# Three of eight K pairs in seven products, with two sums made by a transfer, in the SwiGLU of an encoder block

## The chip, the core and the metric

The kernel runs on one core of a Trainium2 chip. The metric is device time in microseconds of one execution. PE (TensorE) multiplies matrices into PSUM; PEld is its weight load, DVE (VectorE) and ACT (ScalarE) are the two elementwise engines, POOL (GpSimd) and SP (SyncE) are used here mostly to issue transfers (DMAs). Each engine runs its own instructions in order and waits on semaphores for the others.

## The reference

One encoder layer on x of 256 x 2048 in f32: two kinds of attention side by side, cross attention, and a SwiGLU. The change is in the SwiGLU alone:

```python
    hf = rms_norm(x, g_ffn[layer])
    x = x + (jax.nn.silu(hf @ w_gate[layer]) * (hf @ w_up[layer])) @ w_down[layer]
return rms_norm(x, g_final)
```

w_gate and w_up are 2048 x 5632, w_down 5632 x 2048.

## The kernel before

Every f32 product is made from three products in a rounded f32 format (fp32r): each operand is split into a high part (ACT copies with rounding, L97) and a low part (DVE subtracts, L98), and `mm` (L87 to L91) multiplies high by high, high by low and low by high. `split_into` does one split; `weights` and `pair_raw` load weights.

The SwiGLU's 5632 hidden columns are cut into one narrow chunk of 512 and five wide chunks of 1024. They run in three groups (L757), and after each group its part of `w_down` is multiplied and added to the residual `x_res`. Group 0 begins with `narrow_chunk`: the gate product `ga` and the up product `ua` over 16 K tiles, with x^T before normalization (`x2T`); the row factor `rstdf` of the RMS norm is applied afterwards (L731 to L734), and h is transposed on PE (L286).

The wide chunks use x^T after normalization. `normalized_forms` makes it once, after the narrow chunk (L762): it spreads `rstdf` along rows (L692, L693), multiplies the four kept tiles of x^T by it (L697), splits them into `x2n` for plain pairs, and makes `x2f` for the others: four sums and differences of the four 128 x 128 blocks (L714 to L717) and their splits.

A wide chunk makes two wide products, gate and up, with `wide_project`. Each goes over 8 pairs of K tiles in the order `GU_ORDER`. For a plain pair (P) PE makes 8 products of 128 x 128 by 128 x 512, each three matmuls. For a W pair it makes 7 products of sums of blocks (a scheme of Strassen and Winograd): three go straight into the accumulators `accs`, four into PSUM tiles Q1, Q5, Q7 and Q6, which collect over all W pairs of the product and are combined once, after the last W (L677 to L681). Then each accumulator is added to its combination (L684). `accs` take the four banks of `pacc`, Q the four of `pps`, which the transposes also use.

A W pair needs four sums of weight blocks. The weights lie in HBM in the order of blocks 12, 11, 22, 21 (`SUMS`). SP loads the four (1 MB, into `wraw`, three buffers). DVE makes the first two sums in one instruction (L658: blocks 11 and 22, each plus block 12), the others with L662 and L663, all in one tile `tsum` with one buffer. Blocks 11 and 22, block 21, and the first two sums are split into tiles of `wh` and `wl` (four buffers each, handed out in turn, two for a plain pair and three for a W pair); the last two sums into `wh2` and `wl2` (one buffer).

The framework decides the order of instructions on each engine at build time from a simulated timeline (`schedule_with_timeline_sim`, L901), so the built order may differ from the source. Only the weight loads on SP are kept in program order. POOL has no work in the SwiGLU before the last group.

Of the kernel before, what the change touches and what calls it, by code (L numbers as in the profile page):

```python
# [11 lines left out]
F32 = mybir.dt.float32  # L12
# [4 lines left out]
ALU = mybir.AluOpType  # L17
AX = mybir.AxisListType

P = 128  # L20
# [15 lines left out]
NFC = FF // 512  # L36
NPC = (FF - 512) // 1024

GU_ORDER = "PPWPWPPP"

PLAIN, SUMS = ((0, 0), (0, 1), (1, 0), (1, 1)), ((0, 1), (0, 0), (1, 1), (1, 0))
EPS = 1e-6
# [30 lines left out]
def encoder_block(ctx: ExitStack, tc: tile.TileContext, a, out):  # L73
    nc = tc.nc
# [62 lines left out]
    def project(actT, pieces, before=None, fine=0):  # L137

        accs = [pacc.tile([P, 512], F32, name="acc", tag="acc") for _ in range(NT)]
        ncols = pieces[0].shape[2]  # L140
        nk = sum(src.shape[1] for src in pieces)
        kt = 0
        for i, src in enumerate(pieces):
            if before is not None:
                before(i)
            for w in weights(src, i < fine):
                x = actT(kt)
                for tt in range(NT):
                    mm(accs[tt][:, :ncols], x[:, tt * P:(tt + 1) * P], w, start=kt == 0, stop=kt == nk - 1)
                kt += 1  # L150
        return accs
# [211 lines left out]
    for tt in range(NT):  # L363
        c = ckvs[tt]
# [92 lines left out]
    for hg in range(2):  # L457
        t = act_tile(name="mixT")
# [95 lines left out]
    for tt in range(NT):  # L554
        n = nat("xk")
# [53 lines left out]
    wsum = ctx.enter_context(tc.tile_pool(name="wsum", bufs=1))  # L609


    def pair_raw(src):
        raw = wp.tile([P, 2048], F32, name="wraw", tag="wraw", bufs=3)
        raw = raw.rearrange("p (b c) -> p b c", b=4)
        tc.keep_in_program_order(nc.sync.dma_start(out=raw, in_=src))
        return raw

# [6 lines left out]
    def split_blocks(src, pool=None):  # L624
        w = w_tile(src.shape[1], pool)
        split_into(w, src)
        return w

    def wide_project(xk, forms, src, order):

        accs = [[pacc.tile([P, 512], F32, name="acc", tag="acc") for _ in range(2)] for _ in range(NT)]
        used = [[False] * 2 for _ in range(NT)]
        last_w = max(i for i, kind in enumerate(order) if kind == "W")
        first_w = order.index("W")
        Q = {}  # L640
        for i, kind in enumerate(order):
            stop = i == len(order) - 1
            raw = pair_raw(src[i])
            if kind == "P":
                w = [split_blocks(raw[:, 2 * k:2 * k + 2, :]) for k in range(2)]
                for tt in range(NT):
                    for oc in range(2):
                        for k in range(2):
                            mm(accs[tt][oc], xk(2 * i + k)[:, tt * P:(tt + 1) * P], w[k][:, oc, :],
                               not used[tt][oc], stop and k == 1)  # L650
                            used[tt][oc] = True
                continue
            f = forms[i]
            if i == first_w:
                Q = {q: ps_tile(f"q{q}") for q in (1, 5, 7, 6)}
            t = wsum.tile([P, 4, 512], F32, name="tsum", tag="tsum", bufs=1)
            b11 = split_blocks(raw[:, 1:3, :])
            nc.vector.tensor_tensor(out=t[:, 0:2, :], in0=raw[:, 1:3, :],  # L658
                                    in1=raw[:, 0:1, :].to_broadcast([P, 2, 512]), op=ALU.add)
            t13 = split_blocks(t[:, 0:2, :])  # L660
            b21 = split_blocks(raw[:, 3:4, :])
            nc.vector.tensor_tensor(out=t[:, 2, :], in0=t[:, 0, :], in1=raw[:, 2, :], op=ALU.add)  # L662
            nc.vector.tensor_tensor(out=t[:, 3, :], in0=t[:, 2, :], in1=raw[:, 3, :], op=ALU.add)  # L663
            t24 = split_blocks(t[:, 2:4, :], wsum)
            own = i == first_w, i == last_w
            A11, A12, A22, S5, S6, S7, S3 = [f[:, n, :] for n in range(7)]
            mm(Q[1], A11, b11[:, 0, :], *own)
            mm(accs[0][1], S3, b11[:, 1, :], False, stop)
            mm(Q[5], S5, t13[:, 0, :], *own)
            mm(Q[7], S7, t13[:, 1, :], *own)  # L670
            mm(accs[0][0], A12, b21[:, 0, :], False, stop)
            mm(Q[6], S6, t24[:, 0, :], *own)
            mm(accs[1][0], A22, t24[:, 1, :], False, stop)
            if i == last_w:
                res = [act.tile([P, 2, 512], F32, name=f"res{tt}", tag="act") for tt in range(NT)]
                q1, x, v, y = res[0][:, 0, :], res[0][:, 1, :], res[1][:, 0, :], res[1][:, 1, :]
                nc.scalar.copy(out=q1, in_=Q[1])  # L677
                nc.vector.tensor_tensor(out=v, in0=Q[6], in1=q1, op=ALU.subtract)
                nc.vector.tensor_tensor(out=x, in0=Q[5], in1=v, op=ALU.add)
                nc.vector.tensor_tensor(out=v, in0=v, in1=Q[7], op=ALU.subtract)  # L680
                nc.vector.tensor_tensor(out=y, in0=Q[5], in1=v, op=ALU.add)  # L681
        for tt, oc, op in ((0, 0, ALU.add), (0, 1, ALU.add), (1, 0, ALU.subtract), (1, 1, ALU.add)):
            r = res[tt][:, oc, :]
            nc.vector.tensor_tensor(out=r, in0=accs[tt][oc], in1=r, op=op)  # L684
        return res

    def normalized_forms():

        rb = nat("rb")
        rps = ps_tile("rps")  # L690
        for tt in range(NT):
            nc.vector.tensor_copy(out=rb[:, tt * P:(tt + 1) * P], in_=rstdf[:, tt:tt + 1].to_broadcast([P, P]))  # L692
            nc.tensor.transpose(out=rps[:, tt * P:(tt + 1) * P], in_=rb[:, tt * P:(tt + 1) * P], identity=ident)  # L693
        rrow = nat("rrow")
        nc.scalar.copy(out=rrow[:, :S], in_=rps[:, :S])
        for xr in x2raw:
            nc.vector.tensor_tensor(out=xr, in0=xr, in1=rrow[:, :S].unsqueeze(1).to_broadcast([P, 4, S]), op=ALU.mult)  # L697
        plain, forms = {}, {}
        t, n = None, 4
        for i, kind in enumerate(GU_ORDER):  # L700
            xr = x2raw[i // 2]
            ka, kb = i % 2 * 2, i % 2 * 2 + 1
            if kind == "P":
                if n == 4:
                    t, n = act_tile(name="x2n"), 0
                split_into(t[:, n:n + 2, :], xr[:, ka:kb + 1, :])
                plain[2 * i], plain[2 * i + 1] = t[:, n, :], t[:, n + 1, :]
                n += 2
                continue
            f = act_tile((P, 7, P), name="x2f")  # L710
            forms[i] = f
            s = nat("x2s").rearrange("p (n t) -> p n t", n=4)
            a11, a12, a21, a22 = xr[:, ka, :P], xr[:, kb, :P], xr[:, ka, P:], xr[:, kb, P:]
            nc.vector.tensor_tensor(out=s[:, 0, :], in0=a21, in1=a22, op=ALU.subtract)  # L714
            nc.vector.tensor_tensor(out=s[:, 1, :], in0=a11, in1=s[:, 0, :], op=ALU.subtract)
            nc.vector.tensor_tensor(out=s[:, 2, :], in0=a11, in1=a21, op=ALU.subtract)
            nc.vector.tensor_tensor(out=s[:, 3, :], in0=a12, in1=s[:, 1, :], op=ALU.subtract)  # L717
            split_into(f[:, 0:2, :], xr[:, ka:kb + 1, :P])
            split_into(f[:, 2, :], a22)
            split_into(f[:, 3:7, :], s)  # L720
        return plain.__getitem__, forms

    def narrow_chunk(c):

        ga = project(x2T, [a["w_gate0"][0, i] for i in range(4)])
        ua = project(x2T, [a["w_up0"][0, i] for i in range(4)])
        t = act_tile(name="hT")
        for tt in range(NT):
            r = rstdf[:, tt:tt + 1]
            sg = nat("sg")  # L730
            nc.scalar.activation(sg, ga[tt], AF.Sigmoid, scale=r)  # L731
            nc.vector.scalar_tensor_tensor(out=sg, in0=ga[tt], scalar=r, in1=sg, op0=ALU.mult, op1=ALU.mult)
            h = nat("h")
            nc.vector.scalar_tensor_tensor(out=h, in0=ua[tt], scalar=r, in1=sg, op0=ALU.mult, op1=ALU.mult)  # L734
            transposed(t, h, tt, 4)
        return [t]

    def wide_chunk(c):
        g = wide_project(x2n, x2f, a["w_gu"][c, 0], GU_ORDER)
# [18 lines left out]
    for gi, (c0, c1) in enumerate(groups):  # L758
        hT = []
        if gi == 0:  # L760
            hT += narrow_chunk(0)
            x2n, x2f = normalized_forms()  # L762
        for c in range(len(hT) + c0, c1, 2):
            hT += wide_chunk((c - 1) // 2)
        if gi == len(groups) - 1:
            gfb = [act.tile([P, 1024], F32, name="gfb", tag="act") for _ in range(2)]
            for c in range(2):
                nc.gpsimd.dma_start(out=gfb[c],
                                    in_=a["g_final"][:, c * 1024:(c + 1) * 1024].partition_broadcast(P))
        for oc in range(4):  # L770
# [6 lines left out]
            if oc < 3:  # L777
                add_out(project(xT, pieces), oc)
                for tt in range(NT):
# [3 lines left out]
                                            op=ALU.mult)  # L783
# [3 lines left out]
            n = 4 * len(pieces) - 6  # L787
# [117 lines left out]
```

## Time and profile before

| | us |
|---|---|
| median of 3 runs | 1186.28 |
| lowest and highest | 1185.59, 1188.68 |
| the profiled execution | 1185.42 |
| its span | 1183.6 |
| the forms and the join to the first wide chunk, on the timeline | 489 to 504 |
| two wide products without a narrow one, on the timeline | 912 to 997 |

The span is what the trace covers, from first to last instruction; the rest of the execution's time lies around it. A row of the timeline gives start and length in us, engine, line, operation, output and inputs; in brackets the idle time before it and what ended that. A row of a group ends with busy time in all, mean ns of one, and idle time before. The chain that ended last is followed back from the last instruction; its shares say which engine's work made up the time. Matmul ends are modelled, so PE's pace is better read from the starts of matmuls than from their lengths.

### The profile page before, as it was taken

How to read it: one execution, taken by the hardware profiler on the slowest of the kernel's cores; microseconds unless marked ns; L12 is line 12 of the kernel's file. 1: busy time of each engine (PE TensorE's matmuls, PEld its weight loads, DVE VectorE, ACT ScalarE, POOL GpSimd, SP SyncE). 2: the span in 40 equal slices, each digit the busy share in tenths (PEclk: the TensorE clock that was granted, in tenths of full speed). 3: DMA queues.
4: the chain of work that ended last, by engine and by line, in shares of the span. 5: the costliest groups of instructions: out<-in, count | busy, mean ns of one | idle time of the engine just before them, and what ended most of it. 6: DMA issues, size and time to landing. Idle time of an engine off the chain costs nothing.

```text
span 1183.6 us, 14683 instructions
## 1 busy us (share of the span) xinstructions
PE 1160.9 (98%) x5728; PEld 977.3 (83%) x5728; DVE 839.6 (71%) x1084; ACT 593.5 (50%) x830; POOL 66.0 (6%) x83
## 2 busy tenths in 40 slices
PE   8999999999999999799999999999999999999997
PEld 5889888888889988688888888888888887888887
DVE  6768766686867776788755787887546787887553
ACT  5746454454665555455443544544433554554452
POOL 7610000001000000000000000000000000000111
PEclk9999999999999999899999999999999999999999
DMA  8656425445755445445555556555555655755551
GB/s 292 237 181 214 143 107 178 167 154 194 281 201 178 143 147 187 164 148 180 210 209 180 181 207 207 186 179 213 192 199 182 209 178 178 249 180 212 182 207 74
DMA packets 33829, 222.16 MB, mean 188 GB/s; under 512 B 3920, under 2 KB 4304, under 8 KB 9056
## 3 DMA queue, kind: packets, MB, share of 16 engines
q1 hardware_dynamic: 32544, 217.24, 52.2%
q0 software_dynamic: 928, 3.20, 0.9%
q8 instruction: 45, 0.74, 0.2%
q10 hardware_dynamic: 288, 0.79, 0.2%
q14 instruction: 24, 0.20, 0.1%
HBM read 219.11 MB, written 2.10 MB: 187 GB/s over the span
## 4 chain that ended last, share of the span: by engine, by line
PE 94%; DMA 2%; DVE 2%; ACT 1%; issue 1%; SPq 0%; POOLq 0%; POOL 0%; DVEq 0%; ACTq 0%
PE acc L90 28%; PE acc L89 27%; PE acc L91 27%; PE pt L286 2%; PE q L90 2%; PE q L89 2%; PE q L91 2%; DMA wraw<-in_w_in_q 1%; DVE wl L98 1%; DMA xres<-in_x 1%; PE ppt L432 1%; PE psc L91 1%; PE psc L90 1%; PE psc L89 1%; ACT wh L97 0%
## 5 line engine op out<-in xcount | busy, mean ns | idle before, releaser
L98 DVE TENSOR_TENSOR wl<-wraw,wh 128x1024 fp32r<-128x1024 f32 (+2 forms) x399 | 473.6, 1192 | 272.0 <-ACT wh L97 270.5
L97 ACT CAST wh<-wraw 128x1024 fp32r<-128x1024 f32 (+2 forms) x399 | 403.4, 1022 | 466.5 <-PE acc L91 418.1
L90 PE MATMUL acc<-wl,x2n_h 128*128 128x512 f32 x480 | 186.5, 393 | 0.0
L91 PE MATMUL acc<-wh,x2n_l 128*128 128x512 f32 x480 | 185.0, 391 | 0.0
L89 PE MATMUL acc<-wh,x2n_h 128*128 128x512 f32 x480 | 159.3, 393 | 4.1 <-ACT x2n_h L97 2.8
L91 PE MATMUL acc<-wh,hT_l 128*128 128x512 f32 (+1 forms) x352 | 134.1, 381 | 0.0
L90 PE MATMUL acc<-wl,hT_h 128*128 128x512 f32 (+1 forms) x352 | 133.9, 381 | 0.0
L89 PE MATMUL acc<-wh,hT_h 128*128 128x512 f32 (+1 forms) x352 | 133.4, 380 | 0.0
L89 PEld LDWEIGHTS acc<-wh,x2n_h 128*128 128x128 f32 x480 | 90.9, 189 | 23.8 <-ACT x2n_h L97 3.2
L90 PEld LDWEIGHTS acc<-wl,x2n_h 128*128 128x128 f32 x480 | 90.8, 189 | 18.8
L91 PEld LDWEIGHTS acc<-wh,x2n_l 128*128 128x128 f32 x480 | 90.5, 189 | 18.9 <-DVE x2n_l L98 0.3
L90 PE MATMUL acc<-wl,x0T_h 128*128 128x512 f32 (+1 forms) x256 | 98.8, 386 | 2.6 <-DVE wl L98 2.6
L91 PE MATMUL acc<-wh,x0T_l 128*128 128x512 f32 (+1 forms) x256 | 97.6, 382 | 0.0
L89 PE MATMUL acc<-wh,x0T_h 128*128 128x512 f32 (+1 forms) x256 | 94.8, 383 | 2.8 <-ACT wh L97 2.8
L90 PEld LDWEIGHTS acc<-wl,hT_h 128*128 128x128 f32 x352 | 66.2, 188 | 12.4
L89 PEld LDWEIGHTS acc<-wh,hT_h 128*128 128x128 f32 x352 | 66.2, 188 | 12.2
L91 PEld LDWEIGHTS acc<-wh,hT_l 128*128 128x128 f32 x352 | 66.2, 188 | 12.2
L90 PEld LDWEIGHTS acc<-wl,x0T_h 128*128 128x128 f32 x256 | 48.1, 188 | 13.9 <-DVE wl L98 5.8
L89 PEld LDWEIGHTS acc<-wh,x0T_h 128*128 128x128 f32 x256 | 47.5, 188 | 13.1 <-ACT wh L97 4.6
L91 PEld LDWEIGHTS acc<-wh,x0T_l 128*128 128x128 f32 x256 | 48.1, 188 | 8.2
L98 DVE TENSOR_TENSOR wl<-tsum,wh 128x1024 fp32r<-128x1024 f32 x40 | 47.8, 1216 | 0.0
L97 ACT CAST wh<-tsum 128x1024 fp32r<-128x1024 f32 x40 | 41.1, 1046 | 8.7 <-DVE tsum L663 8.5
(332 smaller groups left out, 1843.4 us busy)
## 6 DMA issues: line engine op xcount, KB each, us to landing
wraw<-in_w_gu SPq DMA_DIRECT2D x80, 1024.0 KB, 4.8
wraw<-in_w_down SPq DMA_DIRECT2D x44, 1024.0 KB, 4.8
wraw<-in_w_in SPq DMA_DIRECT2D x24, 1024.0 KB, 4.8
wraw<-in_w_out SPq DMA_DIRECT2D x16, 1024.0 KB, 4.8
wraw<-in_w_xk SPq DMA_DIRECT2D x4, 1024.0 KB, 5.8
wraw<-in_w_xq SPq DMA_DIRECT2D x4, 1024.0 KB, 4.8
wraw<-in_w_xv SPq DMA_DIRECT2D x4, 1024.0 KB, 4.9
wraw<-in_w_xo SPq DMA_DIRECT2D x4, 1024.0 KB, 4.9
```

The source lines that it names most:

```text
L89: nc.tensor.matmul(o, l.h, r.h, start=start, stop=False)
L90: nc.tensor.matmul(o, l.h, r.l, start=False, stop=False)
L91: nc.tensor.matmul(o, l.l, r.h, start=False, stop=stop)
L97: nc.scalar.copy(out=dst.h, in_=src)
L98: last_split[0] = nc.vector.tensor_tensor(out=dst.l, in0=src, in1=dst.h.bitcast(F32), op=ALU.subtract).ins
L286: nc.tensor.transpose(out=pt[:, j * P:(j + 1) * P], in_=src[:, j * P:(j + 1) * P], identity=ident)
L432: nc.tensor.transpose(out=pt[:, kt * S + tt * P:kt * S + (tt + 1) * P], in_=p[:, tt, kt * P:(kt + 1) * P], identity=ident)
```

## The change

- `GU_ORDER` becomes `PPWPWPWP`: seven products for pairs 2, 4 and 6 instead of 2 and 4 (counted from 0). The weights are laid out accordingly, and `normalized_forms` makes three sets of `x2f` and three tiles of plain pairs.
- `normalized_forms` is called between the gate and the up product of the narrow chunk instead of after the chunk. Its instructions so stand ahead of up's in program order; they need `rstdf` and the kept x^T, not the narrow products.
- SP loads only blocks 11, 22 and 21 of a W pair (768 KB). The first two sums are made in a tile of their own, `t13`, by two transfers from POOL: one writes block 12 twice (512 KB), the second adds blocks 11 and 22 on the way (512 KB, with `accum_op`). The second waits for the first, the first for the last reader of the previous `t13`. The last two sums have their own tile `t24`; L662 and L663 stay on DVE, and read `t13` instead of `tsum`. L658 goes.

```diff
-GU_ORDER = "PPWPWPPP"
+GU_ORDER = "PPWPWPWP"
...
     def pair_raw(src):
+        n = src.shape[1]
         raw = wp.tile([P, 2048], F32, name="wraw", tag="wraw", bufs=3)
-        raw = raw.rearrange("p (b c) -> p b c", b=4)
+        raw = raw[:, :n * 512].rearrange("p (b c) -> p b c", b=n)
         tc.keep_in_program_order(nc.sync.dma_start(out=raw, in_=src))
...
-            raw = pair_raw(src[i])
+            raw = pair_raw(src[i] if kind == "P" else src[i, :, 1:4, :])
...
-            t = wsum.tile([P, 4, 512], F32, name="tsum", tag="tsum", bufs=1)
-            b11 = split_blocks(raw[:, 1:3, :])
-            nc.vector.tensor_tensor(out=t[:, 0:2, :], in0=raw[:, 1:3, :],
-                                    in1=raw[:, 0:1, :].to_broadcast([P, 2, 512]), op=ALU.add)
-            t13 = split_blocks(t[:, 0:2, :])
-            b21 = split_blocks(raw[:, 3:4, :])
-            nc.vector.tensor_tensor(out=t[:, 2, :], in0=t[:, 0, :], in1=raw[:, 2, :], op=ALU.add)
-            nc.vector.tensor_tensor(out=t[:, 3, :], in0=t[:, 2, :], in1=raw[:, 3, :], op=ALU.add)
-            t24 = split_blocks(t[:, 2:4, :], wsum)
+            t1 = wsum.tile([P, 2, 512], F32, name="t13", tag="t13", bufs=1)
+            t2 = wsum.tile([P, 2, 512], F32, name="t24", tag="t24", bufs=1)
+            nc.gpsimd.dma_start(out=t1, in_=src[i, :, 0:1, :].to_broadcast([P, 2, 512]))
+            nc.gpsimd.dma_start(out=t1, in_=src[i, :, 1:3, :], accum_op=ALU.add)
+            b11 = split_blocks(raw[:, 0:2, :])
+            t13 = split_blocks(t1)
+            b21 = split_blocks(raw[:, 2:3, :])
+            nc.vector.tensor_tensor(out=t2[:, 0, :], in0=t1[:, 0, :], in1=raw[:, 1, :], op=ALU.add)
+            nc.vector.tensor_tensor(out=t2[:, 1, :], in0=t2[:, 0, :], in1=raw[:, 2, :], op=ALU.add)
+            t24 = split_blocks(t2, wsum)
...
     def narrow_chunk(c):

         ga = project(x2T, [a["w_gate0"][0, i] for i in range(4)])
+        forms = normalized_forms()
         ua = project(x2T, [a["w_up0"][0, i] for i in range(4)])
...
-        return [t]
+        return [t], *forms
...
         if gi == 0:
-            hT += narrow_chunk(0)
-            x2n, x2f = normalized_forms()
+            hT, x2n, x2f = narrow_chunk(0)
```

## The prediction

> **What bounds the kernel now.** I read the page first (busy shares, the chain that ended last), then the busy time of each engine by stretch, then the timeline where PE is not full.
>
> ```profile
> span 1183.6 us, 14683 instructions
> PE 1160.9 (98%) x5728; PEld 977.3 (83%) x5728; DVE 839.6 (71%) x1084; ACT 593.5 (50%) x830; POOL 66.0 (6%) x83
> ...
> PE 94%; DMA 2%; DVE 2%; ACT 1%; issue 1%; SPq 0%; POOLq 0%; POOL 0%; DVEq 0%; ACTq 0%
> ...
> 443.00:467.00 24.00, 24.00 (x115) 19.95 (x114) 16.16 (x21) 12.32 (x17) 0.69 (x1) 1.00 0.57 198
> 467.00:489.00 22.00, 21.99 (x98) 17.87 (x96) 12.39 (x12) 10.51 (x11) 0.00 (x0) 1.00 0.56 196
> 489.00:504.00 15.00, 8.10 (x25) 6.15 (x26) 14.04 (x24) 7.86 (x15) 0.00 (x0) 0.66 0.27 97
> 912.00:997.00 85.00, 85.00 (x375) 70.11 (x374) 62.91 (x68) 41.07 (x45) 0.00 (x0) 1.00 0.57 196
> ...
> 559.09 0.91 PE acc L89 x4
> ```
>
> The chain is 94% PE. The stretches (columns: window, length, then busy time with instruction count of PE, PEld, DVE, ACT, POOL, then PE's granted clock, DMA share, GB/s) show what that means by stage. In two wide products, 912 to 997 us, PE is busy all 85.00 us; DVE has 22.1 us to spare, ACT 43.9. So there a removed matmul is worth its pitch, and a removed DVE instruction nothing by itself. Four matmuls take 0.91 us in the chain: the pitch is 0.2275 us. One stretch is different: from 489 to 504 us PE is busy 8.10 of 15 us at clock 0.66, and DVE 14.04. That is the join of the narrow chunk to the first wide one.
>
> The run that was profiled took 1185.42 us, 1.82 over its span and 0.86 under the median of the three runs shown (1186.28). The sum starts from 1185.42.
>
> **The change, part by part.**
>
> *Three of eight pairs in seven products.* A plain pair is 2x2x2 products of three matmuls, 24; a W pair is 21. There are ten wide products (five wide chunks, gate and up), so the third W removes 30 matmuls: 30 x 0.2275 = **6.8 us**, all on PE, which is full there. It adds no matmul elsewhere.
>
> *The forms beside the up product.*
>
> ```profile
> 488.61 0.39 PE L91 MATMUL acc<-wh,x2T_l 128*128 128x512 f32 x1
> 490.22 0.66 PE L286 MATMUL pt<-ident,h 128*128 128x128 f32 x4 [1.23 <-DVE h L734]
> 493.81 1.12 PE L286 MATMUL pt<-ident,h 128*128 128x128 f32 x4 [2.93 <-DVE h L734]
> 494.71 0.63 PE L693 MATMUL rps<-ident,rb 128*128 128x128 f32 x2
> 498.11 0.80 PE L89 MATMUL acc<-wh,x2n_h 128*128 128x512 f32 x1 [2.76 <-ACT x2n_h L97]
> 503.77 0.39 PE L89 MATMUL acc<-wh,x2n_h 128*128 128x512 f32 x1
> ...
> 496.18 4.62 DVE L697 TENSOR_TENSOR x2T_f<-x2T_f,rrow 128x1024 f32<-128x1024 f32 x4
> L98 DVE TENSOR_TENSOR x2n_l<-x2T_f,x2n_h 128x512 fp32r<-128x512 f32 x6 | 4.1, 680 | 0.0
> 501.32 0.28 DVE L714 TENSOR_TENSOR x2s<-x2T_f 128x128 f32<-128x128 f32 x1
> 502.33 0.61 DVE L98 TENSOR_TENSOR x2f_l<-x2T_f,x2f_h 128x256 fp32r<-128x256 f32 x2
> 509.40 1.28 DVE L98 TENSOR_TENSOR x2f_l<-x2s,x2f_h 128x512 fp32r<-128x512 f32 x2
> ```
>
> The last up matmul starts at 488.61, the first wide one at 498.11, one pitch later than 488.84 if nothing were waited for: 9.27 us. Eight transposes of h (about 0.11 us each, 0.9) and two of rb are real work in it. Then 13 matmuls start between 498.11 and 503.77: 5.66 us where 13 x 0.2275 = 2.96 are due, 2.7 lost to the lower clock. At most 9.27 - 0.9 - 0.2 + 2.7 = 10.9 us can go, if the forms are ready when up ends.
>
> Their DVE work after the change: 4.6 for the four L697, 5 x 0.68 for plain pairs, and for each W 4 x 0.28 + 0.61 + 0.64 = 2.4, three times; 15 us. The rows leave DVE 7.8 us idle in 443 to 467 (about 6 of it after rstdf is known near 448) and 9.6 in 467 to 489, 15.6 together. It just fits, and the forms of late pairs are wanted later still. What ends last then is h: the wide accumulators take the banks of ga and ua, and ua is free only after two L734. The first two accumulators have 12 matmuls (2.7 us) to cover these. I take **9.5 us** as gained, 4 to 10.9 as bounds (4: only the clock and one wait go, because up's weight splits queue behind the forms on DVE).
>
> *The sums by transfer.* Removed from DVE:
>
> ```profile
> L658 DVE TENSOR_TENSOR tsum<-wraw 128x1024 f32<-128x1024 f32 x20 | 24.4, 1219 | 2.6 <-DMA wraw<-in_w_gu 2.2
> L98 DVE TENSOR_TENSOR wl<-tsum,wh 128x1024 fp32r<-128x1024 f32 x40 | 47.8, 1216 | 0.0
> L97 ACT CAST wh<-tsum 128x1024 fp32r<-128x1024 f32 x40 | 41.1, 1046 | 8.7 <-DVE tsum L663 8.5
> ```
>
> 1.22 us in each W; DVE was not the limit, so zero, but with it a third W costs DVE 5.6 us instead of 6.9 beside 4.8 of PE. Added: two POOL transfers of 512 KB for each of 30 Ws, the second waiting for the first. No row shows an accumulating transfer; the nearest are the plain ones from POOL and SP.
>
> ```profile
> L768 POOL DMA_DIRECT2D gfb<-in_g_final x2: 530/554/577, 1007.1 to 1011.4; - x2
> ...
> DMA to landing us min/median/max: 4.8/5.2/5.6
> ...
> L547 POOL DMA_DIRECT2D mn<-in_mem x4: 537/546/645, 293.1 to 294.8; - x4
> ...
> DMA to landing us min/median/max: 6.0/6.9/10.6
> ...
> wraw<-in_w_ukv_v SPq DMA_DIRECT2D x2, 512.0 KB, 3.4
> wraw<-in_w_gu SPq DMA_DIRECT2D x80, 1024.0 KB, 4.8
> wraw<-in_w_gu SPq DMA_DIRECT2D x3, 1024.0 KB, 7.7
> ```
>
> The tile of the first two sums has one buffer. So a W's first transfer waits until the previous W's t13 was split (and L662 has read it); then come transfer, transfer, cast (1.05), subtraction (1.22): one link C = D1 + D2 + 2.4 with hops. Plain POOL transfers of this size take 5.2 (g_final, two alone) to 6.9 (four at once). I take 5.2 + 5.2 for the two, C = 12.8, because g_final's are issued as singly as these will be and in the same stage; bounds 3.4 + 3.4 (C = 9.2) and 6.9 + 10.6 (C = 19.9). Behind a late accumulation wait, in order, the cast of t13 on ACT and L662 on DVE with every split behind them, and raw's buffer, so SP's next load. On POOL nothing else is queued in this stage (0.00 busy in the row above).
>
> Is there room for C?
>
> ```profile
> 922.54 1.22 DVE L98 TENSOR_TENSOR wl<-tsum,wh 128x1024 fp32r<-128x1024 f32 x1
> 923.69 0.40 PE L89 MATMUL acc<-wh,x2f_h 128*128 128x512 f32 x1
> 932.16 0.39 PE L89 MATMUL q<-wh,x2f_h 128*128 128x512 f32 x1
> 932.39 0.39 PE L90 MATMUL acc<-wl,x2n_h 128*128 128x512 f32 x1
> 934.20 0.39 PE L89 MATMUL acc<-wh,x2f_h 128*128 128x512 f32 x1
> 938.60 0.40 PE L91 MATMUL acc<-wh,x2f_l 128*128 128x512 f32 x1
> 942.53 0.68 DVE L681 TENSOR_TENSOR res<-q,res 128x512 f32<-128x512 f32 x1
> ```
>
> t13 of the first W is split (922.54) just as that W's matmuls begin (923.69). A W takes 4.78 us of PE, a plain pair 5.46. In source order the third W asks for its t13 after 2 x 10.24 + 6 x 0.2275 = 21.8 us, and two links lie in that: **C may be 10.9**. But the built order is not the source order: at 932.16 a product of the second W stands among those of the plain pair (932.39). Sums in one PSUM bank may come in any order, and the plain pairs need no t13. If the 12 matmuls of the last W that need sums (2.7 us) go to the end of the product, two links have 30.7 - 2.7 = 28.0 us: **C may be 14.0**. The first W of a product has 10.9 us more and is never late.
>
> I take the second, since 12.8 lies below 14.0 and the trace shows such interleaving; left over, 0.4 us in each product where the combination of the Qs ends later (last W matmul 938.60, L681 at 942.53, so 4.6 us after it, beside the 5.46 of the one plain pair that is now left): 10 x 0.4 = **4 us**, bounds 0 and 12. The extra traffic (a W moves 1.75 MB instead of 1) raises a DMA share of 0.57 to some 0.75; next to g_final's transfers a weight load took 7.7 instead of 4.8, still inside two pairs of prefetch.
>
> The Trainium skill, DMA: Bandwidth & Descriptors, section "Anatomy of one DMA — SWDGE (gpsimd) path", fits a POOL transfer as 2.0 us plus bytes over 436 GB/s. That estimates 3.2 us for each of these, C near 8.8, and no wait in any order: the sum would be 1169. The trace's 4.8 to 10.6 does not agree, so this case is not counted on.
>
> **Sum**: 1185.4 - 6.8 - 9.5 + 4 = **1173 us**.
>
> **The rivals.**
>
> *The two transfers set the pace (slower).* If the order stays near the source's, or the order was laid for shorter transfers, each product waits 2C - 21.8. With C = 12.8 that is 3.8 us, ten times 38: 1185.4 - 16.3 + 38 = **1207**. With g_final's least (4.8 + 4.8, C = 12.0) 1191; with 5.2 + 6.0, the least of mem's, C = 13.6 and 1223. It turns to a loss when 20 x (C - 10.9) passes 16.3, at C = 11.7. For it: every plain POOL pair in the trace sums to 9.6 or more, above the 8.5 that C = 10.9 leaves, and an accumulation can hardly be quicker. Against: the interleaving.
>
> *Part of the wait is hidden (no change).* A wait of 1.3 to 2 us in each product eats both gains: **1186**.
>
> *The forms do not hide.* If the forms push up's splits or h back, only 6.8 us and some of the clock remain: **1179**. For it: DVE has 15.6 us for 15.
>
> **How the numbers follow.** Hidden, 1173: 0.42, with a range of its own of 1167 to 1180 (forms 10.9 and no tail; forms 4). Forms do not hide, 1179: 0.08. Eaten up, 1186: 0.12. Transfers set the pace, 1207 (1191 to 1223): 0.38. Faster by over 0.3% (3.6 us, about what a measurement can tell from no change) 0.50, within it 0.12, slower 0.38. As both signs hold much, the range runs from 1167 to 1223; a transfer slower than 11.2 us for the pair lies beyond.
>
> **What would show it.** Right: PE busy throughout 487 to 500 us at clock 1.00; 30 fewer matmuls; t13's cast never waiting for a transfer for long; from one wide chunk's start to the next about 1.4 us less. Wrong: waits of PE on casts or splits whose own wait is the accumulated tile, twenty times 1 to 3 us, a PE clock under 1.00 in the wide stage, and accumulating transfers that take over 6 us. If DVE shows 22 us full beside up and PE waits there for weight splits, the forms were the wrong step.

## The result and the profile after

The changed kernel takes 1331.53 us (median of 4 runs, 1327.68 to 1335.03) beside 1186.47 for the kernel before in the same comparison: a ratio of 1.1219, 95% interval 1.1183 to 1.1254. It is 145 us slower; 1173 was forecast, and the range ended at 1223.

From the page of the changed kernel: span, busy time, the chain that ended last, two groups, and the transfers with their median time to landing.

```profile
span 1325.9 us, 14790 instructions
PE 1205.8 (91%) x5698; PEld 992.9 (75%) x5698; DVE 849.0 (64%) x1110; ACT 606.1 (46%) x852; POOL 113.4 (9%) x143
...
PE 25%; DMA 23%; DVE 8%; issue 3%; ACT 1%; POOL 0%; DVEq 0%; POOLq 0%; ACTq 0%
DMA t<-in_w_gu 23%; PE acc L89 8%; PE acc L91 8%; PE acc L90 8%; DVE wl L98 4%; ACT wh L97 1%; DVE t L664 1%; DVE res L686 1%; PE q L89 1%; PE q L90 1%; DVE t L665 1%; PE q L91 1%; DVE res L748 0%; DVE res L680 0%; DVE res L681 0%
...
L89 PE MATMUL q<-wh,x2f_h 128*128 128x512 f32 x120 | 53.8, 503 | 96.2 <-ACT wh L97 96.2
L664 DVE TENSOR_TENSOR t<-t,wraw 128x512 f32<-128x512 f32 x30 | 20.8, 693 | 187.1 <-DMA t<-in_w_gu 183.6
...
t<-in_w_gu POOLq DMA_DIRECT2D x60, 512.0 KB, 7.1
```

(`t` is the tile the transfers write; L659 issues the first transfer and L660 the accumulating one, L664 and L665 are the remaining sums.) The chain was 94% PE before; now PE has 25% of the span and the two transfers have 23%. PE's idle time (span less busy) is 120.1 us where it was 22.7, so 97.4 more. Its busy time is 44.9 more with 30 matmuls (6.8 us) fewer, so the matmuls themselves cost 51.7 more. These two make up the longer span.

The waits, as sum, count and longest, of all engines:

```profile
POOL t L659 <- DVE wl L98: 494.5, 29, 99.1
...
POOL t L660 <- DMA t<-in_w_gu: 215.1, 29, 9.7
...
DVE t L664 <- DMA t<-in_w_gu: 183.6, 23, 10.3
ACT wh L97 <- DMA t<-in_w_gu: 131.0, 20, 10.2
PEld q L89 <- ACT wh L97: 105.7, 22, 6.1
PE q L89 <- ACT wh L97: 96.2, 20, 5.7
```

Read from the bottom: PE waits 20 times, 4.8 us in the mean, for the cast of a W's first two sums; ACT's cast and DVE's L664 wait for the accumulating transfer; that waits on POOL for the first transfer; and the first waits until DVE has split the previous W's sums. It is a ring. Twenty is two for each of ten products: from the first W to the second and from the second to the third. Three plain pairs lie between a product's last W and the next one's first, and there PE does not wait.

POOL's timeline in one product shows how long the ring is:

```profile
561.86 0.73 POOL L659 DMA_DIRECT2D t<-in_w_gu  x1 [13.13 <-DVE wl L98]
569.27 0.87 POOL L660 DMA_DIRECT2D t<-in_w_gu  x1 [6.67 <-DMA t<-in_w_gu]
578.60 0.73 POOL L659 DMA_DIRECT2D t<-in_w_gu  x1 [8.46 <-DVE wl L98]
586.72 0.88 POOL L660 DMA_DIRECT2D t<-in_w_gu  x1 [7.38 <-DMA t<-in_w_gu]
596.33 0.73 POOL L659 DMA_DIRECT2D t<-in_w_gu  x1 [8.73 <-DVE wl L98]
```

From one first transfer to the next it is 16.7 and 17.7 us (17.3 in the mean of all such steps). PE needs 4.78 + 5.46 = 10.24 for the W and the plain pair between. About 7 us are late twenty times: some 140.

What PE loses beside the wait, on its timeline after one of them:

```profile
576.93 1.22 PE L89 MATMUL q<-wh,x2f_h 128*128 128x512 f32 x2 [5.19 <-ACT wh L97]
...
579.85 0.63 PE L91 MATMUL q<-wh,x2f_l 128*128 128x512 f32 x1
580.27 0.63 PE L90 MATMUL q<-wl,x2f_h 128*128 128x512 f32 x1
...
581.55 0.40 PE L91 MATMUL acc<-wh,x2f_l 128*128 128x512 f32 x1
```

After the wait of 5.19 us matmuls start 0.43 to 0.51 apart instead of 0.2275 (the granted clock is 0.50), and the ten from 576.93 to 581.55 take 4.62 us instead of 2.28. So this wait costs 2.3 us more, and the next one, at 594.56, 2.1. At that rate twenty cost an estimated 45; that is most of the 51.7. The Trainium skill, TensorE: Matmul & The Clock Gate, section "Part 1: The HAM clock gate (the "warmup" mystery)", says that the array falls to half its clock after an idle window of about 3.4 us and returns after about as long of sustained work. The half pace agrees with these rows; the return took 4.6 us here, and about 3 to 6 us after the other waits of this kernel.

### The profile page after: what moved, and what is told of

Its sections match the earlier page's. It is cut to its first block, busy times and chain, and to the rows that moved or that the text cites. A ratio compares the mean times of both kernels' runs of the same rounds, so it can differ in the third digit from the quotient of the medians.

```text
span 1325.9 us, 14790 instructions
## 1 busy us (share of the span) xinstructions
PE 1205.8 (91%) x5698; PEld 992.9 (75%) x5698; DVE 849.0 (64%) x1110; ACT 606.1 (46%) x852; POOL 113.4 (9%) x143
## 4 chain that ended last, share of the span: by engine, by line
PE 25%; DMA 23%; DVE 8%; issue 3%; ACT 1%; POOL 0%; DVEq 0%; POOLq 0%; ACTq 0%
DMA t<-in_w_gu 23%; PE acc L89 8%; PE acc L91 8%; PE acc L90 8%; DVE wl L98 4%; ACT wh L97 1%; DVE t L664 1%; DVE res L686 1%; PE q L89 1%; PE q L90 1%; DVE t L665 1%; PE q L91 1%; DVE res L748 0%; DVE res L680 0%; DVE res L681 0%
## 5 line engine op out<-in xcount | busy, mean ns | idle before, releaser
L90 PE MATMUL acc<-wl,x2n_h 128*128 128x512 f32 x400 | 156.3, 391 | 0.0
L91 PE MATMUL acc<-wh,x2n_l 128*128 128x512 f32 x400 | 155.9, 391 | 0.0
L89 PE MATMUL q<-wh,x2f_h 128*128 128x512 f32 x120 | 53.8, 503 | 96.2 <-ACT wh L97 96.2
L664 DVE TENSOR_TENSOR t<-t,wraw 128x512 f32<-128x512 f32 x30 | 20.8, 693 | 187.1 <-DMA t<-in_w_gu 183.6
L97 ACT CAST wh<-t 128x1024 fp32r<-128x1024 f32 x60 | 62.8, 1046 | 145.3 <-DMA t<-in_w_gu 131.0
L89 PEld LDWEIGHTS q<-wh,x2f_h 128*128 128x128 f32 x120 | 24.9, 227 | 109.0 <-ACT wh L97 105.7
L89 PEld LDWEIGHTS acc<-wh,x2n_h 128*128 128x128 f32 x400 | 78.7, 202 | 35.4 <-ACT wh L97 9.4
L91 PEld LDWEIGHTS acc<-wh,x2n_l 128*128 128x128 f32 x400 | 75.3, 188 | 16.7
L90 PEld LDWEIGHTS acc<-wl,x2n_h 128*128 128x128 f32 x400 | 75.6, 189 | 16.0
L98 DVE TENSOR_TENSOR wl<-t,wh 128x1024 fp32r<-128x1024 f32 x60 | 73.2, 1220 | 3.4 <-ACT wh L97 3.4
```

The costliest lines, as they stand in the source:

```text
L89: nc.tensor.matmul(o, l.h, r.h, start=start, stop=False)
L90: nc.tensor.matmul(o, l.h, r.l, start=False, stop=False)
L91: nc.tensor.matmul(o, l.l, r.h, start=False, stop=stop)
L97: nc.scalar.copy(out=dst.h, in_=src)
L98: last_split[0] = nc.vector.tensor_tensor(out=dst.l, in0=src, in1=dst.h.bitcast(F32), op=ALU.subtract).ins
L664: nc.vector.tensor_tensor(out=t2[:, 0, :], in0=t1[:, 0, :], in1=raw[:, 1, :], op=ALU.add)
```

## The experiments

Ratios are to the kernel before, in the same comparison (its medians there: 1183.5 to 1185.3). e3, e4 and e5 rest on two runs each.

| run | what | us | ratio (95%) |
|---|---|---|---|
| e1_forms | forms moved only | 1174.57 | 0.9902 (0.9873 to 0.9931) |
| e2_third_w | and a third W, sums on DVE | 1183.45 | 0.9981 (0.9966 to 0.9996) |
| e3_two_w | changed kernel, two Ws | 1243.73 | 1.0488 (1.0442 to 1.0534) |
| e4_plain | second transfer not accumulating | 1292.65 | 1.0900 (1.0860 to 1.0941) |
| e5_two_buffers | two buffers for `t13` | 1241.17 | 1.0477 (1.0444 to 1.0510) |
| e6_middle | middle W's sums on DVE | 1241.47 | 1.0483 (1.0467 to 1.0498) |
| e7_earlier | e2 in the order PWPWPWPP | 1171.18 | 0.9886 (0.9870 to 0.9903) |
| e8_half_loads | half the plain pairs' weights | 1321.21 | one run |
| e9_no_broadcast | first transfer reads plainly | 1321.58 | one run |
| e10_first_only | transfers for the first W only | 1206.05 | 1.0181 (1.0135 to 1.0226) |
| e11_first_only_earlier | same, PWPWPWPP | 1202.72 | 1.0135 (1.0105 to 1.0164) |
| e12_spaced | two Ws, PWPPPWPP | 1202.71 | 1.0134 (1.0103 to 1.0166) |
| e13_spaced_behind | e12, sums later on DVE | 1176.34 | 0.9928 (0.9904 to 0.9953) |
| e14_first_behind | e11, sums later on DVE | 1169.64 | 0.9875 (0.9848 to 0.9902) |
| e15_two_buffers_behind | e5, sums later on DVE | 1196.32 | 1.0111 (1.0093 to 1.0129) |
| e16_changed_behind | changed kernel, sums later | 1332.48 | one run |
| e17_unread | e7 with transfers nobody reads | 1171.05 | 0.9888 (0.9861 to 0.9915) |
| e18_all_behind | e15 in the order PWPWPWPP | 1170.36 | 0.9886 (0.9871 to 0.9900) |

### The parts without the transfers

e1 is the kernel before with only the call of `normalized_forms` moved; e2 adds the third W, with L658 and all sums still on DVE.

```diff
 # e1_forms
         ga = project(x2T, [a["w_gate0"][0, i] for i in range(4)])
+        forms = normalized_forms()
 # e2_third_w: e1, and
-GU_ORDER = "PPWPWPPP"
+GU_ORDER = "PPWPWPWP"
```

> The kernel before with the forms alone moved beside the up product (two W pairs, all sums on DVE). The join alone is changed, so this gives the term of 9.5 us by itself: 1175 to 1178 by the prediction's step. If up's weight splits are held back by the forms, 1180 or more. It bears on no theory of the loss except that the forms have no part in it: any time above 1190 would say that they have.

> The changed kernel with the sums on DVE as before (no transfer by POOL): forms moved, three W pairs. Theory CHAIN (the loss of 145 us is the chain from the last reader of the one t13 buffer through two POOL transfers to the next split): the loss is gone and both gains stand, 1168 to 1176. Theory LOAD (the third W itself, its DVE work of 6.9 us beside 4.8 of PE and the Q combination beside one plain pair): still well above before, 1200 or more. Theory TRAFFIC (weight loads held up by the added bytes): also fast here, 1168 to 1176, so it does not tell CHAIN from TRAFFIC.

The forms give 10.7 us (1185.25 to 1174.57). The third W gives nothing here: e2 is 8.9 slower than e1, where 6.8 faster was due, and lies between what the theories expected (1168 to 1176, or 1200 and more). Its waits of PE, then busy time by stretch (PE, PEld, DVE, ACT, POOL, clock, DMA share, GB/s):

```profile
PE acc L89 <- DVE res L684: 9.2, 10, 2.6
```
```profile
955.00:1040.00 85.00, 82.92 (x371) 67.59 (x369) 76.03 (x86) 45.76 (x51) 0.00 (x0) 1.00 0.56 198
```

PE waits once in each product for L684, the last addition of the product before, because the next product's accumulators take the same banks. With the last W one pair from the end, its combination (L678 to L681) and the additions meet on DVE, 76.03 busy of 85. e7 moves the same three Ws one pair forward:

```diff
-GU_ORDER = "PPWPWPWP"
+GU_ORDER = "PWPWPWPP"
```

> Three W pairs with all sums on DVE, at pairs 1, 3 and 5 (order PWPWPWPP) instead of 2, 4 and 6. If the third W's missing gain lies in the end of the product (Q combination and evictions on DVE beside a single plain pair), two plain pairs there give it back: 1167 to 1172. If it lies in DVE's total (6.9 us for a W) the place does not matter: 1180 to 1186.

```profile
955.00:1040.00 85.00, 85.00 (x382) 70.08 (x381) 78.38 (x90) 47.23 (x54) 0.00 (x0) 1.00 0.57 197
```

In the same stretch of e7 PE is full, with DVE busier than in e2. So it was the place of the last W and not DVE's amount of work: 12.3 us for the order alone, of which the waits for L684 show 9.2, and 3.4 less than e1, half of the 6.8. So of the 145 us the forms are -10.7, the third W in its place +8.9, and the transfers the rest: 1331.5 - 1183.5 = 148.

### What makes the ring long

```diff
 # e3_two_w: the changed kernel, and
-GU_ORDER = "PPWPWPWP"
+GU_ORDER = "PPWPWPPP"
 # e4_plain: what is left out is block 12 in the first two sums
-            nc.gpsimd.dma_start(out=t1, in_=src[i, :, 1:3, :], accum_op=ALU.add)
+            nc.gpsimd.dma_start(out=t1, in_=src[i, :, 1:3, :])
 # e9_no_broadcast
-            nc.gpsimd.dma_start(out=t1, in_=src[i, :, 0:1, :].to_broadcast([P, 2, 512]))
+            nc.gpsimd.dma_start(out=t1, in_=src[i, :, 0:2, :])
 # e8_half_loads: plain pairs
-            raw = pair_raw(src[i] if kind == "P" else src[i, :, 1:4, :])
+            raw = pair_raw(src[i, :, 0:2, :] if kind == "P" else src[i, :, 1:4, :])
```

> The changed kernel with two W pairs (2 and 4). CHAIN: one tight link a product instead of two, so less than half of the loss: with a link of 17.3 us and 11.6 of room, 5.7 us and some of PE's slower clock after the wait, ten times: 1235 to 1260. TRAFFIC: two thirds of the added bytes, two thirds of the loss: 1280 to 1295. LOAD: no loss, about 1176.

> The changed kernel with a plain second transfer in place of the accumulating one (the sums of block 12 with 11 and 22 are left out; every wait and every byte from HBM stays). CHAIN, with the accumulation as its long part: the second transfer falls from 6.5 us to 4.8 to 5.2, a link from 17.3 to about 15.8, and 20 links give back 25 to 35 us: 1295 to 1307. If the accumulation costs nothing by itself and it is the two transfers in a row: 1320 to 1332.

> The changed kernel with its first transfer reading two blocks as they lie (512 KB read) instead of block 12 twice (256 KB read, written twice); what is computed is left out in that the first two sums get other blocks. If the doubled reading is what makes the first transfer take 7.8 us in place of the 5.2 forecast: 5 to 6 us here, a link of some 15 us and 1290 to 1310. If it is not: 7.5 to 8 us and 1325 to 1337.

> The changed kernel with half of each plain pair's weights loaded and used twice (the other half of those weights is left out of the result): every wait of the chain stays, but 512 KB less cross the DMA engines in each plain pair. If crowding with the weight loads makes the first transfer 7.8 us instead of the 5.2 of g_final's, it falls to 5.5 to 6.5 here, and 20 links give 20 to 45 us: 1285 to 1312. If it is the form of the transfer (block 12 written twice in rows of 2 KB), it stays at 7.5 to 8 and the time at 1320 to 1332.

One tight step in each product (e3) costs 69 us against e1, two cost 148 against e2: about 7 for each of ten and of twenty. Without accumulation (e4) the second transfer lands in 4.7 us instead of 6.5 in the median (first transfer 7.9 instead of 7.8), and the time falls by 38.9: 20 x 1.8 = 36, a little more than was expected. These are the rows of time to landing, in the changed kernel for the first and the accumulating transfer, and in e4 for the second:

```profile
DMA to landing us min/median/max: 4.9/7.8/10.1
...
DMA to landing us min/median/max: 6.0/6.5/8.0
```
```profile
DMA to landing us min/median/max: 4.0/4.7/5.9
```

The form of the first transfer and its neighbours brought less time. Both runs below are single ones, and the changed kernel's own runs lie 7 us apart. Read plainly (e9) the first lands in 6.7, but the second in 7.1; together 0.5 less, and 10 us less, as 20 x 0.5 gives. With half of the plain pairs' weights (e8) the first lands in 6.3 and a tight step takes 15.9 us in the mean instead of 17.3, yet only 10 us are gained where 20 x 1.4 = 28 were due. The step from one product's last W to the next one's first became longer there (28.4 us instead of 22.7 between the first two products), and PE waited 18.6 us for DVE's splits of weights instead of 3.0; why was not followed.

### Fewer tight steps

```diff
 # e6_middle: the changed kernel, and for the W at place 4
+            if i == 4:
+                nc.vector.tensor_tensor(out=t1, in0=raw[:, 1:3, :],
+                                        in1=raw[:, 0:1, :].to_broadcast([P, 2, 512]), op=ALU.add)
...
 # e5_two_buffers: the changed kernel, and (with nat's buffers cut from 7 to 5 for room)
-            t1 = wsum.tile([P, 2, 512], F32, name="t13", tag="t13", bufs=1)
+            t1 = wsum.tile([P, 2, 512], F32, name="t13", tag="t13", bufs=2)
 # e12_spaced: the changed kernel, and
-GU_ORDER = "PPWPWPWP"
+GU_ORDER = "PWPPPWPP"
 # e10_first_only: e6 with "if i != first_w"; e11_first_only_earlier: that, in the order PWPWPWPP
```

> The changed kernel with the middle W's first two sums on DVE and the other two by transfer (one buffer). CHAIN: links now span 20.5 us of PE inside a product and 21 across products, against 17.3 needed, so neither waits for the transfer by much; what is left is the third W's own cost at the product's end (8.9 us above the forms alone when all sums were on DVE), eased by two L658 less: 1172 to 1190. TRAFFIC: two thirds of the bytes, so a loss of 70 us or more: 1245 or more.

> The changed kernel with two buffers for the first two sums (the pool of row tiles goes from 7 to 5 to make room). CHAIN, by the one buffer: a W's transfers no longer wait for the previous W's last reader; the pairs still run one behind the other on POOL (7.8 + 6.5 = 14.3 us a pair, 43 for three beside 41.6 of PE in a product), so most of the loss goes: 1185 to 1215, and POOL's wait for the reader falls from the longest to the shorter one. TRAFFIC: the bytes are the same and more crowded: 1290 or more.

> The changed kernel with two W pairs in each product, at places 1 and 5 (PWPPPWPP), so that each W is followed by three plain pairs before the next one, in the product and across products: 4.78 + 3 x 5.46 = 21.2 us from W to W. The same transfers and the same bytes as the kernel with two Ws at places 2 and 4 (1243.7 us). CHAIN (transfer, accumulating transfer, cast, subtraction on one buffer, 16.7 to 17.7 us measured, is too long for two Ws 10.2 us apart): 21.2 is longer than 17.7, so hardly a wait is left and the time is 1166 to 1182. LOAD (the added traffic or the slower accumulation slow the whole stage): the same bytes, so 1225 to 1250 again.

> Three Ws (PPWPWPWP), the first two sums by transfers for the first W of each product alone, by VectorE for the other two; still one buffer, and the other Ws load all four blocks. The only link with transfers is then from the last W of a product to the first W of the next, with three plain pairs between: 4.78 + 3 x 5.46 = 21.2 us. CHAIN: no link is tight, 1174 to 1187 (the kernel with three Ws and all sums on VectorE took 1183.5). If any use of the transfers costs by itself: above 1195.

> The same with the three Ws at places 1, 3 and 5 (PWPWPWPP), so that two plain pairs follow the last W. With all sums on VectorE this order took 1171.2 us. CHAIN: 1167 to 1173, no worse, and at best a few us less because VectorE has 1.2 us less to do for each product. If any use of the transfers costs by itself: above 1180.

e6 missed, for a reason that can be read in its code: the middle W's sums lie in the same one buffer, so the step from it to the last W is as tight as before. One tight step was left and cost 58 us over e2, where e3's cost 69. Its time alone can't be told from what the traffic would give (1245 or more); PE's waits for the cast, about one in each product, speak for the ring:

```profile
PE q L89 <- ACT wh L97: 30.5, 11, 4.4
```

e12 is the clean case: the transfers and bytes of e3, each W three plain pairs from the next. It takes 41 us less than e3. But it, e10, e11 and e5, all without a tight step, missed what the ring alone would give: they stayed 23 to 58 us over their counterparts with sums on DVE (e1, e2, e7 and e2; e1 has e12's two Ws in other places). The ring is a cause, and not the only one. DVE's timeline in e12 at a product's end shows the other:

```profile
527.92 0.69 DVE L683 TENSOR_TENSOR res<-q,res 128x512 f32<-128x512 f32 x1
532.44 0.69 DVE L664 TENSOR_TENSOR t<-t,wraw 128x512 f32<-128x512 f32 x1 [3.83 <-DMA wraw<-in_w_gu]
533.05 1.22 DVE L98 TENSOR_TENSOR wl<-wraw,wh 128x1024 fp32r<-128x1024 f32 x1
...
535.92 0.68 DVE L686 TENSOR_TENSOR res<-acc,res 128x512 f32<-128x512 f32 x1
```

DVE stands 3.83 us at L664, a sum of the next product's first W, whose weights have not landed; the splits and L686, the addition that frees PE's banks, are behind it. The build orders DVE by a simulated timeline, in which the data had presumably come by then; that timeline is not on record. Over e12's whole run these waits of DVE are:

```profile
DVE t L664 <- DMA t<-in_w_gu: 44.5, 9, 7.0
DVE t L664 <- DMA wraw<-in_w_gu: 32.1, 10, 5.0
```

### Queue or traffic

The rival for this rest was the traffic: in e11 a W's weights land in 7.2 us, a plain pair's in 4.9. To tell the two apart, the sums were pinned behind ready work on DVE, with every transfer kept (e13, e14; e16 for the changed kernel); and the traffic was added to e7 with nobody waiting for it (e17).

```diff
 # e13 = e12, e14 = e11, e15 = e5, e16 = the changed kernel, each with
+            behind = [last_split[0]] + (last_res if i == first_w else [])
...
+            with ExitStack() as es:
+                for ins in behind:
+                    es.enter_context(tc.issue_after(ins))
                 nc.vector.tensor_tensor(out=t2[:, 0, :], in0=t1[:, 0, :], in1=raw[:, 1, :], op=ALU.add)
                 nc.vector.tensor_tensor(out=t2[:, 1, :], in0=t2[:, 0, :], in1=raw[:, 2, :], op=ALU.add)
 # e17_unread = e7, and for the first W
+                c = nc.gpsimd.tensor_copy(out=gate, in_=raw[:, 0, 0:1])
+                with tc.issue_after(c.ins):
+                    nc.gpsimd.dma_start(out=t1, in_=src[i, :, 0:1, :].to_broadcast([P, 2, 512]))
+                    nc.gpsimd.dma_start(out=t1, in_=src[i, :, 1:3, :], accum_op=ALU.add)
```

(`last_res` is the last L686 of the product before.)

> The kernel with two Ws 21.2 us apart (PWPPPWPP, 1202.7 us) with the two remaining sums of a W (they read the accumulated tile) queued on VectorE behind the splits of the plain pair before it, and for the first W of a product also behind the last addition of the previous product. Transfers and bytes are the same. QUEUE (the builder expects the transfers sooner than they land, so these sums stand early in VectorE's order and hold back splits and additions that are ready): 1166 to 1185. LOAD (the added traffic delays the weight loads of the W pairs, whatever the order): 1197 to 1206.

> The same queueing in the kernel that makes only the first W's sums by transfers, in the order PWPWPWPP (1202.7 us; 1171.2 with all sums on VectorE). QUEUE: 1166 to 1180. LOAD: 1197 to 1206.

> The kernel with all sums on VectorE in the order PWPWPWPP (1171.2 us), with the two transfers added for the first W of each product into a tile that nobody reads, issued when that W's weights have landed: the traffic without anyone who waits for it (two buffers of the small tiles fewer, for room). QUEUE: 1169 to 1178. LOAD: 1195 to 1210.

> The changed kernel (1331.5 us) with the same queueing. CHAIN with QUEUE: the two tight links of each product stay, so PE still waits twenty times for the cast of the accumulated tile and the time is 1285 to 1335. If the order on VectorE alone made the loss: below 1230.

All four came out as the queue says. e13 is 26.4 us under e12 and e14 33.1 under e11; the unread transfers changed nothing (1171.05 beside 1171.18). In e17 the weights still landed in 4.8 us, so it says nothing of late loads; in e14 they are as late as in e11 (a W's in 7.0 us), and 33.1 us are gone all the same. In e13 the stretch from 504 to 554 us reads

```profile
504.00:554.00 50.00, 50.00 (x222) 41.20 (x221) 35.28 (x39) 24.76 (x27) 3.22 (x4) 1.00 0.79 248
```

PE is full at clock 1.00 with a DMA share of 0.79 and 248 GB/s, more than in e12's same stretch:

```profile
504.00:554.00 50.00, 48.81 (x213) 39.65 (x213) 34.51 (x39) 24.49 (x28) 3.21 (x4) 1.00 0.73 231
```

So the traffic is not what was paid for. And where the ring is tight, the queue is no cure (e16):

```profile
PE q L89 <- ACT wh L97: 101.0, 20, 6.5
```

### Both cures together

e15 is e5 with the sums behind; e18 is e15 in the order PWPWPWPP.

> The changed kernel, in its own order PPWPWPWP, with two buffers for the accumulated tile (1241.2 us) and with the two remaining sums queued on VectorE behind the splits of the plain pair before them. Without a tight link and without early places in VectorE's order both causes are gone: 1172 to 1195, near the kernel with the same order and all sums on VectorE (1183.5). If the three pairs of transfers follow each other too slowly on GpSimd (each second transfer waits there for its first): 1205 or more, with waits of PE on the cast of the accumulated tile.

> The same in the order PWPWPWPP: all 30 pairs of sums by transfers, two buffers, the remaining sums queued later. If both causes are gone: 1163 to 1178 (all sums on VectorE: 1171.2; transfers for the first W alone: 1169.6). If GpSimd's row of transfers sets the pace: 1195 or more.

e15 takes 45 us off e5 and ends just above its expected range, 13 over e2. DVE still waits for the transfers a little, and POOL stands at the second of each pair:

```profile
DVE t L670 <- DMA t<-in_w_gu: 30.3, 8, 5.1
```
```profile
POOL t L663 <- DMA t<-in_w_gu: 258.4, 30, 12.5
```

The three pairs of a product follow each other on POOL there, and the last W is still one pair from the end; which of the two makes the 13 was not separated. With the Ws one pair earlier (e18) PE waits for none of it; these are its two longest waits:

```profile
PE acc L90 <- DVE wl L98: 2.9, 5, 1.1
PE acc L89 <- ACT wh L97: 2.4, 5, 1.0
```

It takes 1170.36, 1.1% faster than the kernel before, with all 30 pairs of sums by transfer. But e7, with no transfer at all, takes 1171.18, and e14 1169.64: the transfers bring 1.5 us at most, less than the intervals of the ratios can tell apart.

## Why the prediction was wrong, point by point

- **What bounds the kernel: right.** PE was full, and DVE's 1.22 us for each W were worth nothing by themselves: e18, e14 and e7 lie within 1.5 us.
- **The forms: right.** 9.5 forecast, 10.7 measured in e1, near the stated most of 10.9. The stretch that was 8.10 busy at clock 0.66 is full in the changed kernel:

```profile
489.00:504.00 15.00, 15.00 (x71) 12.41 (x70) 13.23 (x18) 8.94 (x13) 0.00 (x0) 1.00 0.47 166
```

- **The third W: wrong by its end.** The 6.8 us were taken whole with a tail of 4 (0 to 12) for the later combination; no row gave its 0.4 us for each product, as the 4.6 for the combination lay below the pair's 5.46. Measured in e2 the tail is 6.8 + 8.9 = 15.7, beyond its bound. The prediction weighed the combination alone against the one plain pair left; what came late was L684 behind it, in one queue with the next pairs' splits, and the next product's banks with it. One pair more of distance (e7) takes back 12.3.
- **The length of a link C: mis-sized, and the step that failed.** "I take 5.2 + 5.2 for the two, C = 12.8" was measured as 7.8 + 6.5, and a ring of 16.7 to 17.7. The 2.4 for cast and subtraction was 2.85: in the product above DVE's wait for the sums ended at 575.75 and the next first transfer was issued at 578.60, as L664 and L665 stood on DVE ahead of the split. The value of 5.2 came from g_final's transfers, said to be issued singly and in the same stage; but they read one row of 4 KB for all partitions (`partition_broadcast`), not 512 KB of weights. Of the first transfer's 2.6 us too much, 1.1 go when it reads plainly (e9) and 1.5 when fewer weights are loaded beside it (e8), in single runs that were not combined; the accumulating one costs 1.8 more than a plain one (e4). A nearer row was used for a bound only: mem's transfers do read 512 KB, and with their median of 6.9 for both, C would have been 16.2. The bounds (9.2 to 19.9) held it; the range did not use them. It was drawn from 12.0 to 13.6 for the rival.
- **The room: the choice fell too.** "I take the second, since 12.8 lies below 14.0" needed PE's order to put the last W's matmuls at the end of a product. The built order did not do so: in the product above, the first matmul with the last W's sums starts at 594.56 and the product goes on to 605.8, 11 us and not 2.7. Even 14.0 would not have held 17, so it is C that takes the time out of the range.
- **The price of the sums by transfer, put at nothing: two prices.** The ring is the larger; the wait in order on DVE, which the prediction named ("Behind a late accumulation wait, in order, ... L662 on DVE with every split behind them") but gave no price, is by itself 26 to 33 us where the ring is loose.
- **The rival "two transfers set the pace": the mechanism, right, at too small a price.** Its formula 2C - 21.8 gives 12.6 for a product with C = 17.2, so 126 and, from 1185.4 - 16.3, 1295. For the rest to 1331 there are the third W's end (15.7 in e2) and what the formula lacked, PE's half pace after each wait; as the ring goes on during those slow matmuls, the 45 us lie partly inside the 126 and can't simply be added, and the two were not separated.
- **What would show it: right.** It named twenty waits of PE behind the accumulated tile, a clock under 1.00 and accumulating transfers over 6 us. They are 4.8 us each instead of 1 to 3, the mean clock is 0.955 (0.994 before), and the transfers take 6.0 to 8.0.
- **The estimate from the Trainium skill.** From the fit in the Trainium skill, DMA: Bandwidth & Descriptors, section "Anatomy of one DMA — SWDGE (gpsimd) path", an estimate of 3.2 us was worked out for such a transfer. No transfer of the changed kernel agrees: the quickest of the 60 landed in 4.9.

## What to carry to other kernels

A tile with one buffer that a chain of transfers fills is a ring: add up its whole length (issue, landing, cast, subtraction, next issue), take each landing from the crowded stage and not the quietest row, and compare it with the time between two uses. An instruction that waits for a transfer should stand in its engine's order behind all work that is ready before the transfer really lands, since a build that orders by a simulated timeline can put it ahead of work that PE needs. And the place of a costly step within a loop can be worth more than the step: one pair of distance from the product's end brought 12 us, the transfers 1.5 at most.

## What the runs showed of the hardware that was not expected

- An accumulating transfer of 512 KB from POOL costs 1.8 us more to land than the same one without (6.5 us in the changed kernel and 4.7 in e4, in the median), and its issue holds POOL 878 ns instead of 552.
- Transfers that nobody waits for took part in a DMA share of 0.70 (e17, from 504 to 554 us; 0.61 in e7) at no cost to PE, and with 40 transfers waited for late PE was full at 248 GB/s (e13), though a 1 MB weight load then landed in 6.8 us instead of 4.8.
- A wait of PE of about 5 us is followed by about 3 to 6 us at half pace (granted clock 0.50 from 576.93 to 581.55 us): it costs nearly half as much again as its length.
